# Four small transfers at the head of a matmul with batch norm: 256 words of w, or 64 of w and 64 of x

## The chip, the cores and the metric

The kernel runs on one core of one Trainium2 chip. The metric is the device time of one execution in microseconds, the median of several. The engines are TensorE (PE, its weight loads PEld), VectorE (DVE), ScalarE (ACT), GpSimd (POOL) and SyncE (SP). SyncE, ScalarE and GpSimd can each issue DMA transfers from a queue of their own; sixteen DMA engines carry out what all queues hold.

## The reference

`x` is 16 x 512 x 1024, `weight` (w below) is 1024 x 768, both float32 in HBM; gamma and beta have 768 elements.

```python
y = np.matmul(x, weight)
mean = np.mean(y, axis=(0, 1), keepdims=True)
var = np.var(y, axis=(0, 1), keepdims=True)
y_norm = (y - mean) / np.sqrt(var + eps)
return (gamma * y_norm + beta).astype(np.float32)
```

The statistics go over all 8192 rows, for each of the 768 columns. So no value can be stored before all of its column has been multiplied.

## The kernel before

**Tiling.** The 8192 rows of x are 16 chunks of 512 rows; the 768 columns are six tiles of 128. The contraction of 1024 is cut into four quarters of 256. Quarter `i` of w lies on partitions `32*i` to `32*i+31`, as bfloat16; each partition holds `JW` = 4 groups (`jw`) of two neighbouring rows of w. x is loaded the same way: `load_x` (L395) sends one transfer for each quarter of the contraction, to the 32 partitions of that quarter, and VectorE turns the data with STREAM_TRANSPOSE (L428, L435) so that TensorE can contract over the partitions. Both kinds of load convert float32 to bfloat16 on the way and go through GpSimd's queue.

**Order.** Most work is emitted as tasks with a due time; `arrange` (L122) puts them into one order for each engine with estimated durations, and `seq` (L293) pins that order. The loads come in a list written by hand (L440): `("x", 0), ("w", 0, 2), ("x", 1), ("w", 2, 4)`, the next two pieces of 256 rows of x, then whole chunks of 512 rows. `BETWEEN = {0: [0, 1]}` moves the first two quarters of the first w piece ahead of the x quarters of the first piece. So GpSimd issues: quarters 0 and 1 of w (`jw` 0 and 1, that is the first 128 rows of each 256), four quarters of x rows 0 to 255, quarters 2 and 3 of w, four quarters of x rows 256 to 511, four quarters of w (`jw` 2 and 3), and so on. The first eight are issued at once; each later one waits for the landing of an earlier transfer. A w transfer is 64 packets and an x transfer of 256 rows is 256, over the sixteen DMA engines.

**The first products.** TensorE begins with idle matmuls (L591, L594) that fill its time. The first product (L510, columns 0 to 255, x as the stationary operand) needs the first piece of x, turned, and all four quarters of the first w piece. Then L575 multiplies with w stationary. The next products need x rows 256 to 511, and after them the second w piece.

**The lines of the change.** Ahead of all tasks the kernel fills a few constants with VectorE, lets ScalarE compute one square root (L346, which loads ScalarE's function table), and issues four small transfers from SyncE (L347 to L350) into the tile `touched`, which nothing reads:

```python
seq(nc.scalar.activation(warm, eps_sb, AF.Sqrt))
touched = singles.tile([P, 2, TOUCH], f32)
first_rows = weight.rearrange("(i jw c e) n -> i c jw (e n)", i=4, jw=JW, e=2)
for i in range(4):
    seq(nc.sync.dma_start(touched[32 * i:32 * i + 32, 0:2], first_rows[i, :, 0:2, 0:TOUCH]))
```

Each of the four reads 64 single words of one quarter of w: word 0 of every second row of that quarter's first 128 rows. These are the rows that the first w piece begins its descriptors with. `load_quarter` (L386) issues the transfers of w proper, with the same arrangement.

Of the kernel before, what the change touches and what calls it, by code (L numbers as in the profile page):

```python
# [227 lines left out]
def kernel(  # L228
# [9 lines left out]
    nc = tc.nc  # L238
    f32 = mybir.dt.float32
# [8 lines left out]
    P = 128  # L248
# [7 lines left out]
    JW = KQ // 64  # L256
# [4 lines left out]
    TOUCH = 1  # L261
# [20 lines left out]
    x_flat = x.flatten_outer_dims()  # L282
    out_flat = out.flatten_outer_dims()

    singles = ctx.enter_context(tc.tile_pool(name="singles", bufs=1))
# [7 lines left out]
    def seq(bi):  # L293

        ins = bi.ins
        prev = last.get(ins.engine)
        if prev is not None:
            tc.add_manual_dep(
                ins, prev,
                mybir.DependencyInfo(mybir.DependencyClass.NoSync, mybir.DependencyReason.DATA),  # L300
                reason="order",
            )
        last[ins.engine] = ins.name
        return bi
# [38 lines left out]
    base = singles.tile([P, 2], f32)  # L343
    fss = singles.tile([P, 2], f32)

    seq(nc.scalar.activation(warm, eps_sb, AF.Sqrt))  # L346
    touched = singles.tile([P, 2, TOUCH], f32)  # L347
    first_rows = weight.rearrange("(i jw c e) n -> i c jw (e n)", i=4, jw=JW, e=2)
    for i in range(4):
        seq(nc.sync.dma_start(touched[32 * i:32 * i + 32, 0:2], first_rows[i, :, 0:2, 0:TOUCH]))  # L350


    tasks, turns = [], {}
# [88 lines left out]
    at = M - CH  # L442
# [5 lines left out]
    for kind, n, *n1 in order:  # L448
# [24 lines left out]
        for i in range(rows // QR):  # L473
            c, q = divmod(m0 // QR + i, QPC)
# [9 lines left out]
        if rows % QR:  # L484
            t0 = rows // QR * QR // 32
            m1 = m0 + 32 * t0
            c, q = divmod(m1 // QR, QPC)
# [851 lines left out]
    for c, r0, rows in ends:  # L1339
        due = E + 2.0 + 0.6 * c  # L1340
        n = max(rows // CH, 1)
# [70 lines left out]
```

## Time and profile before

| what | value |
|---|---|
| median of 3 runs (lowest to highest) | 205.74 us (205.7 to 206.15) |
| span of the profiled execution | 204.1 us |
| its own end-to-end time | not given; the median is 1.64 us above the span |
| PE busy, share of the span | 189.3 us, 93% |
| DVE, ACT, POOL busy | 159.3, 146.2, 124.1 us |
| granted TensorE clock, mean | 0.979 |
| queue q0 (GpSimd's loads): packets, MB | 34624, 18.36 |
| queue q1 (SyncE's transfers): packets, MB | 63920, 30.16 |
| the four small transfers, issue to landing | 1.6 to 4.1 us, median 2.6 |

Times are from one profiled execution. Bytes are counted as they are written, so a load that converts to bfloat16 counts half of what it reads. A chain of waits follows the end of the kernel back, at each step to what released the waiting work. In the timeline a row has its start, its length, the engine, the line, the operation and how many of them it merges; in brackets stands the idle time before it and what ended it.

### The profile page before, as it was taken

The numbers are of one execution on the slowest core, as the hardware profiler recorded it, in microseconds if no ns is written. First come the engines' busy times: TensorE is split into PE (matmuls) and PEld (weight loads), VectorE is DVE, ScalarE is ACT, GpSimd is POOL, SyncE is SP. The second block draws the span as 40 slices with busy tenths as digits, with TensorE's granted clock in tenths as the row PEclk, the third lists the DMA queues.
The fourth block names the chain that finished last, engine by engine and source line by source line (L and its number), as shares of the span: only waits on it lengthen the run. The fifth ranks groups of instructions, "written<-read, shape, count | busy, mean of one in ns | idle before, by whom it ended". The sixth has DMA issues, their size and how long they took to land.

```text
span 204.1 us, 3510 instructions
## 1 busy us (share of the span) xinstructions
PE 189.3 (93%) x1210; PEld 114.5 (56%) x1210; DVE 159.3 (78%) x250; ACT 146.2 (72%) x260; POOL 124.1 (61%) x150
## 2 busy tenths in 40 slices
PE   7969999999999999999999999999999999997900
PEld 3457554657488888777865444444444445544600
DVE  4031879999999999969989998987999878657900
ACT  2001461368989999899978766999998959956950
POOL 7776954877499989997403999389613312940000
PEclk9999999999999999999999999999999999999965
DMA  4999999999999999999686899899999999999998
GB/s 71 172 199 196 176 196 196 196 197 197 190 193 197 197 196 196 196 197 195 103 181 200 297 339 336 248 301 328 295 322 227 336 303 274 347 343 310 310 347 253
DMA packets 98562, 48.74 MB, mean 239 GB/s; under 512 B 24304, under 2 KB 98032, under 8 KB 98544
## 3 DMA queue, kind: packets, MB, share of 16 engines
q0 software_dynamic: 34624, 18.36, 65.5%
q1 hardware_dynamic: 63920, 30.16, 52.6%
q8 instruction: 9, 0.15, 0.3%
q14 instruction: 9, 0.07, 0.1%
HBM read 36.71 MB, written 25.17 MB: 303 GB/s over the span
## 4 chain that ended last, share of the span: by engine, by line
PE 86%; ACT 3%; DMA 3%; POOL 2%; issue 1%; ACTq 0%; DVE 0%; POOLq 0%
PE y_ps L575 54%; PE y_ps L510 24%; PE y_ps L814 4%; ACT o_sb L1361 3%; DMA ring<-in_x_dram 3%; PE o_ps L1044 1%; POOL ring L403 1%; POOL w_sb L387 1%; PE y_ps L753 1%; PE a_ps L903 1%; PE o_ps L1074 0%; ACTq L1407 0%; PE idle_ps L591 0%; PE tot_ps L871 0%; ACT ring L1252 0%
## 5 line engine op out<-in xcount | busy, mean ns | idle before, releaser
L575 PEld LDWEIGHTS <-w_sb 128*128 128x128 bf16 x520 | 50.3, 97 | 57.6
L575 PE MATMUL y_ps<-xT_sb,w_sb 128*128 128x512 bf16 (+1 forms) x272 | 59.3, 371 | 0.0
L575 PE MATMUL y_ps<-x_pl,w_sb 128*128 128x512 bf16 x248 | 57.4, 379 | 0.0
L403 POOL DMA_DIRECT2D ring<-in_x_dram x76 | 47.2, 626 | 14.4 <-DMA ring<-in_x_dram 5.5
L510 PE MATMUL y_ps<-w_sb,xT_sb 128*128 128x256 bf16 x448 | 50.6, 273 | 1.7 <-DMA ring<-in_x_dram 1.6
L510 PEld LDWEIGHTS <-xT_sb 128*128 128x128 bf16 x448 | 43.5, 98 | 9.4 <-DVE xT_sb L435 2.9
L435 DVE STREAM_TRANSPOSE xT_sb<-ring 128x1024 f32<-128x1024 f32 (+1 forms) x29 | 31.2, 1111 | 14.1 <-DMA ring<-in_x_dram 13.9
L711 DVE BATCH_NORM_STATS2 stats<-y_ps 128x6 f32<-128x512 f32 x46 | 30.9, 687 | 7.7 <-PE y_ps L575 7.2
L715 ACT CAST y_sb<-y_ps 128x512 bf16<-128x512 f32 x51 | 29.0, 593 | 10.4 <-DVE stats L711 6.3
L547 ACT COPY x_pl<-xT_sb 128x1024 bf16<-128x1024 bf16 x32 | 32.8, 1063 | 1.7 <-DVE xT_sb L435 1.7
L942 POOL TENSOR_TENSOR ring<-ring,sum 128x1024 f32<-128x1024 f32 (+1 forms) x11 | 23.8, 2188 | 14.9 <-ACT y_ps L724 10.9
L659 ACT ACTIVATE sq_sb<-y_ps 128x512 f32<-128x512 f32 x28 | 16.3, 610 | 16.2 <-PE y_ps L510 15.9
L666 POOL TENSOR_TENSOR sum<-sum,sq_sb 128x512 f32<-128x512 f32 x20 | 25.6, 1278 | 3.0 <-ACT sq_sb L659 1.7
L662 DVE TENSOR_TENSOR sum<-y_ps,sum 128x512 f32<-128x512 f32 x28 | 18.9, 675 | 6.3 <-ACT sq_sb L659 5.3
L672 ACT CAST y_sb<-y_ps 128x512 bf16<-128x512 f32 x28 | 16.3, 594 | 8.2 <-DVE sum L662 8.0
L1178 POOL TENSOR_TENSOR ring<-ring,sum 128x1024 f32<-128x1024 f32 x6 | 14.8, 2477 | 9.8 <-issue 8.5
L937 DVE TENSOR_TENSOR ring<-y_sb,a_ps 128x1024 f32<-128x1024 bf16 (+1 forms) x16 | 16.7, 1079 | 0.1
L1044 PE MATMUL o_ps<-ident,y_sb 128*128 128x128 bf16 x104 | 13.1, 221 | 1.6 <-DVE y_sb L1348 1.5
L1232 ACT CAST ring<-ring 128x1024 f32<-128x1024 bf16 x13 | 13.8, 1063 | 0.6 <-DMA ring<-y_sb 0.6
L1145 POOL COPY sum<-sum 32x256 f32<-32x256 f32 (+1 forms) x17 | 5.8, 340 | 13.4 <-DVE sum L1142 6.5
L428 DVE STREAM_TRANSPOSE xT_sb<-ring 128x2048 bf16<-128x2048 bf16 x6 | 13.5, 2290 | 0.1
L591 PE MATMUL idle_ps<-idle_sb 128*128 128x512 f32 x18 | 9.6, 688 | 1.5 <-DVE idle_sb L316 1.5
(104 smaller groups left out, 153.7 us busy)
## 6 DMA issues: line engine op xcount, KB each, us to landing
out_dram<-ring SPq DMA_DIRECT2D x37, 512.0 KB, 3.4
ring<-in_x_dram POOLq DMA_DIRECT2D x52, 256.0 KB, 8.8
out_dram<-o_sb SPq DMA_DIRECT2D x6, 512.0 KB, 4.7
ring<-in_x_dram POOLq DMA_DIRECT2D x16, 128.0 KB, 5.9
w_sb<-in_weight_dram POOLq DMA_DIRECT2D x8, 192.0 KB, 6.2
out_dram<-ring SPq DMA_DIRECT2D x6, 256.0 KB, 3.0
ring<-in_x_dram POOLq DMA_DIRECT2D x4, 192.0 KB, 7.8
out_dram<-o_sb SPq DMA_DIRECT2D x3, 256.0 KB, 2.5
```

The source lines that it names most:

```text
L403: bi = seq(nc.gpsimd.dma_start(x_bf[32 * i:32 * i + 32], src[:, :, KQ * i:KQ * (i + 1)]))
L435: seq(nc.vector.transpose(dst, src[:, :, jw0:jw1]))
L510: seq(nc.tensor.matmul(y_ps[:, s], x_of(c, jw, e, t * P, (t + 1) * P), w_sb[:, jw, e, 0:NA], start=(s == 0 and jw == 0 and e == 0), stop=( ...
L547: seq(nc.scalar.copy(dst, pairs) if eng == "ACT" else ENG[eng].tensor_copy(dst, pairs))
L575: seq(nc.tensor.matmul(y_ps, w_sb[:, jw, e, nt * P:(nt + 1) * P], moving(c, jw, e, q0 * QR, q1 * QR, parted), start=(jw == 0 and e == 0 an ...
L659: seq(nc.scalar.activation(sq_sb[:, 0:n], slot.tile[:, 0:n], AF.Square))
L662: seq(nc.vector.tensor_add(sum1, slot.tile[:, 0:n], sum1))
L666: seq(ENG[eng].tensor_add(acc, acc, state["sq"][:, 0:n]))
L711: seq(nc.vector.bn_stats(dst, slot.tile))
L715: seq(nc.scalar.copy(y(nt, c), slot.tile))
L937: seq(nc.vector.tensor_mul(slot.o, y_row[c].y[:, s0:s1], aff[0][:, None, :].to_broadcast([P, n, NA])))
L942: seq(ENG[eng].tensor_add(slot.o, slot.o, row[:, None, :].to_broadcast([P, n, NA])))
```

## The change

The four small transfers from SyncE go. In their place come two, issued before ScalarE's square root: SyncE reads 64 words of w and ScalarE's own queue 64 words of x, each into one column of the first 64 partitions of `touched`. In both, the words are word 0 of every sixteenth row of rows 0 to 1023: for w that is the whole matrix (48 KB from word to word), for x the first two chunks (64 KB from word to word). The rearrangement sets the sixteen steps within a block of 256 rows (`e`) outermost and the four blocks (`h`) inside. Nothing reads `touched` in either kernel.

```diff
@@ -343,11 +343,11 @@
     base = singles.tile([P, 2], f32)
     fss = singles.tile([P, 2], f32)
 
+    touched = singles.tile([P, 2], f32)
+    for eng, src, at in ((nc.sync, weight, 0), (nc.scalar, x_flat, 1)):
+        words = src[0:1024, 0:1].rearrange("(h e s) n -> e h (s n)", h=4, e=16)
+        seq(eng.dma_start(touched[0:64, at:at + 1], words[:, :, 0:1]))
     seq(nc.scalar.activation(warm, eps_sb, AF.Sqrt))
-    touched = singles.tile([P, 2, TOUCH], f32)
-    first_rows = weight.rearrange("(i jw c e) n -> i c jw (e n)", i=4, jw=JW, e=2)
-    for i in range(4):
-        seq(nc.sync.dma_start(touched[32 * i:32 * i + 32, 0:2], first_rows[i, :, 0:2, 0:TOUCH]))
```

## The prediction

> **What bounds the kernel now.** I read the chain of waits first, because it says which work the end can be followed back to, then the timeline of the head, then the head in windows of 0.5 us, and last the single DMA packets and landings in the trace. The chain, cut to its first 30 us (start, length, what):
>
> ```profile
> 5.98 6.13 DMA ring<-in_x_dram
> 12.11 0.03 issue
> 12.14 1.03 PE y_ps L510 x8
> ...
> 14.99 0.86 PE idle_ps L591 x2
> 15.85 0.87 PE y_ps L510 x8
> 16.72 1.81 PE y_ps L575 x16
> 18.54 0.07 issue
> 18.61 1.91 PE y_ps L510 x16
> ```
>
> From 12.14 us to 184.8 us nearly every later piece of the chain is TensorE work, back to back. Ahead of it stands the wait for the loads. So two clocks rule: until 18.6 us TensorE goes on only as transfers land (at 12.14, 15.68 and 18.61), and from then on as fast as it can multiply. A microsecond won or lost in the landings of the head is a microsecond of the whole kernel, as long as every later landing moves with it. It does: the load queue always has up to eight transfers outstanding, and GpSimd issues each next one about 0.3 us after the oldest has landed (8.38 after 8.09, 9.06 after 8.77, 9.80 after 9.51).
>
> The timeline of the head, with what the change touches (start, length, engine, line):
>
> ```profile
> 0.73 1.28 ACT L346 ACT_TABLE_LOAD   x1 [0.73 <-PEq L1393]
> 0.74 1.81 SPq L350 DMA_DIRECT2D touched<-in_weight_dram  x4
> 1.30 1.21 POOL L387 DMA_DIRECT2D w_sb<-in_weight_dram  x2 [0.85 <-POOLq L1393]
> 2.51 2.29 POOL L403 DMA_DIRECT2D ring<-in_x_dram  x4
> 4.79 1.06 POOL L387 DMA_DIRECT2D w_sb<-in_weight_dram  x2
> 7.00 0.30 ACT L457 CAST ident<-ident 128x128 f32<-128x128 bf16 x1 [4.77 <-POOL ident masks.py:199]
> 10.26 1.30 DVE L435 STREAM_TRANSPOSE xT_sb<-ring 128x512 f32<-128x512 f32 x2 [7.13 <-DMA ring<-in_x_dram]
> ```
>
> No instruction reads `touched`, so the four small transfers can act only through the DMA engines and HBM. The eight large ones behind them are two quarters of w, four of x, two of w. In the trace they land at 4.99, 6.02; 8.09, 8.77, 9.51, 10.14; 11.06, 12.01 us. The transposes begin 0.12 us after the fourth quarter of x, and TensorE 0.13 us after the last quarter of w. Except at the third of them, x quarters follow each other by 0.63 to 0.74 us and w quarters by 0.92 to 1.03. The first quarter of x comes 2.07 us after the w quarter before it, about 1.4 more than its like. The windows show the same hole (the last number is GB/s, the one before it the DMA share):
>
> ```profile
> 5.50:6.00 0.50, 0.50 (x2) 0.19 (x1) 0.00 (x0) 0.00 (x0) 0.50 (x3) 1.00 1.35 167
> 6.00:6.50 0.50, 0.50 (x2) 0.19 (x1) 0.00 (x0) 0.00 (x0) 0.50 (x2) 1.00 0.59 64
> 6.50:7.00 0.50, 0.50 (x3) 0.24 (x2) 0.00 (x0) 0.00 (x1) 0.42 (x3) 1.00 1.04 118
> 7.00:7.50 0.50, 0.50 (x3) 0.26 (x2) 0.00 (x0) 0.30 (x1) 0.48 (x1) 1.00 1.30 169
> 11.00:11.50 0.50, 0.00 (x0) 0.00 (x0) 0.50 (x1) 0.00 (x0) 0.15 (x1) 1.00 1.43 197
> ```
>
> Eleven microseconds in, x streams at 197 GB/s; when x is read for the first time it runs at 64 to 169 for 2 us. This is what a word of x, read ahead, could take away.
>
> **The change, part by part.**
>
> Issue slots. SyncE issues one transfer where it issued four of 0.40 to 0.43 us: 1.2 us less, worth nothing, because its next transfer waits tens of microseconds for DVE (46.2 us in the waits of its queue). ScalarE gets one DMA issue ahead of its table load, about 0.41 us by the four SyncE rows; the table load and the `warm` activation move from 0.73–2.2 to about 1.15–2.65 us. The cover is ScalarE's idle time until 7.00, of which 4.77 us are a wait for `ident`; some 4.3 us of it are left. Without that cover it would cost 0.41. At the end of the kernel one more queue may have to be waited for; a semaphore wait there takes 0.02 to 0.05 us, below what can be seen.
>
> Removed words. Touches three and four are underway during the first two w quarters: 160 of their packets, 8 data words and 2 completions an engine, start after 2.55 us. The sixteen engines finish the two quarters 0.96 us apart with them, and the last two w quarters 0.94 us apart without them. So taking them away is worth 0.00 to 0.04 us; I take 0. What they warm: the old words sit on every second row of the first 128 rows of each w quarter, the new ones on every sixteenth row of all of w. The second halves of the quarters have no touch at all now, and their packets take 247 to 248 ns when first read, as in the steady state. So a sparser cover of w should cost nothing.
>
> The first w packets. Twelve packets that begin between 2.69 and 3.14 us take 460 to 992 ns instead of 247, although words of their rows had been read by 2.54 us. That is some 0.6 us lost, and the w touch does not prevent it. In the changed kernel nothing is queued beside these packets. The price of this part lies between −0.6 (the third touch stood in their way) and +0.6 (more of them, should the thinner cover matter); I take 0, since nothing in the first two touches differs from what stays.
>
> The x words. They leave ScalarE at about 0.74 us. The first SyncE touch had its first packet 1.0 us after its issue and landed at 2.32 us, so the x words are done by about 2.4, before the first w packet at 2.69. If the first read of x is what is dear, it is paid there, where no load is yet moving. What that brings, from three rows. (a) One engine lags: of the sixteen completions of the first x quarter fifteen come by 6.66 and the last at 8.09; this engine stays 0.55 us behind the others up to the landing at 12.01 (the others by 11.45). If only its lag goes, 0.55 us. (b) Mean loss: against 195 GB/s the four windows miss 28 + 131 + 77 + 26 = 262 GB/s over 0.5 us each, 131 KB, which is 0.67 us of streaming. (c) All of the slip goes: the first x quarter then lands with its fifteen early engines, at about 6.7, 1.4 us sooner, and the last w quarter at 10.6; the fillers of TensorE end at 10.56, so all 1.4 would be used. I take (b), 0.67 us: fifteen engines passed the first x quarter without delay and stalled in the second, which reads the same rows, so I doubt that a touch cures the whole.
>
> The sum: 0 for the issue slots, 0 for the w words, 0 for the first w packets, −0.67 for x. The profiled execution spans 204.1 us; its own end-to-end time is not given, and 205.74 − 204.1 = 1.64 us lie around the span, which nothing here touches. The median becomes 205.74 − 0.67 = 205.07, so 205.1 us.
>
> **A rule against it.** In the trace the stall has the size of 0.1 to 0.7 us on single 512-byte packets (371, 738 and 693 ns are the longest, against 60). The Trainium skill, HBM Reference, Latency, knows no dearer first access: 0.2 us on average, 2 us at high load. By that rule there is nothing to warm, the hole is a matter of load, and the sum would be 0 (205.7 us). The recovery to 197 GB/s under the same load speaks against it; the stall on packets of rows already being read speaks for it. I carry its consequence as the first rival.
>
> **The rivals.**
>
> Nothing to warm (0.27). The hole at 6 us is not a first read. For: fifteen engines got through the first x quarter in 0.7 us, and a similar hole stands at 22.5 to 24.5 us, where 39 packets of x are slow, while rows 256 to 1023, first read in between, show none. Against: the first slow packet, at 5.28 us, is one of the first of x, and nothing else in the records starts there (GpSimd's `ident` work begins at 5.84). The result is 205.7, within 0.2% (0.41 us, about what a measurement of this kernel can tell from no change).
>
> The x words block w (0.20, slower). A slow read holds an engine for both queues: between 2.54 and 3.51 us only one packet of the touches moves while the first w packets crawl. If the x words meet what the lagging engine met, 1.4 us, they hold their engines from 1.75 to about 3.2, 0.5 us into the w packets; and if the hole at 6 us stays all the same, the kernel ends 0.5 later, at 206.25. It decides for this when the x words land after 2.7 us and the first x quarter still follows its w quarter by 2 us. Against: the w touches, just as new, took 0.25 us for 80 packets.
>
> The thinner w cover matters (0.08, slower). The third and fourth w quarters, whose words were touched on their own rows, would then begin with packets of 0.8 us: +0.6, 206.3. The untouched half quarters at 247 ns speak against it.
>
> **How the numbers follow.** The forecast, that x is warmed, has 0.45, with its own range 204.3 (c) to 205.2 (a). Faster by over 0.2% means below 205.33: all of this case. Within 0.2% is the first rival, 0.27; slower the other two, 0.28. The range must hold eight in ten: it takes the forecast from (c), 204.3, through the first rival and up to the slow cases at 206.25 and 206.3. What is left out is a gain in both the x hole and the first w packets together (below 204) and a slow case with a dearer stall than any here.
>
> **What would show it.** Right: the x words land by about 2.5 us; the windows between 5.5 and 7.5 us show over 150 GB/s throughout; the first x quarter follows its w quarter by under 1.4 us instead of 2.07; TensorE's first L510 matmul starts near 11.5 instead of 12.14, and the matmuls at 15.68 and 18.61 come as much earlier. Wrong: the hole stays at 64 GB/s near 6 us with the first matmul at 12.1 (nothing to warm); first w packets beginning after 2.7 or a first w landing after 5.0 (blocked); slow packets at the third w quarter (thin cover); or a head that is 0.67 earlier while a later wait, for the x rows that land at 24.3 us, gives it back.

## The result: slower by 0.9 us, and the profile after

The changed kernel takes 206.8 us (median of 17 runs, 206.42 to 208.33) against 206.06 us for the kernel before (17 runs); the ratio is 1.0043, 95% interval 1.0028 to 1.0057, so about 0.9 us (0.6 to 1.2); the two medians alone are 0.74 apart. A later set on one chip gave 207.06 against 205.82, ratio 1.0061 (1.0040 to 1.0082). The forecast was a gain of 0.67 us, to 205.1: wrong in sign. The profiled execution after spans 204.7 us (run of 206.52), that of before 204.1. One execution of an experiment below, the profiled one of the kernel in plain order, took 291.7 us at a granted clock of 0.65 and is left out of the ratio; of its trace only the landings of the head, SyncE's stop and the drain are read.

The chain of waits of the changed kernel, first 30 us (start, length, what):

```profile
5.32 6.85 DMA w_sb<-in_weight_dram
12.17 0.28 issue
12.45 6.18 DMA w_sb<-in_weight_dram
18.64 0.28 issue
18.92 5.87 DMA ring<-in_x_dram
24.80 0.03 issue
...
26.22 1.92 PE y_ps L510 x16
```

In the chain of the kernel before, the same products stand at 25.93:

```profile
25.93 1.92 PE y_ps L510 x16
```

Two things are to be seen. The last w quarter lands at 12.17 instead of 12.01. And the start of TensorE's unbroken work, 25.93 us before, is now 26.22, when a piece of x has landed at 24.80 and has been turned. From there to 184 us the products stay 0.29 or 0.30 us late.

The timeline of the head (start, length, engine, line, operation):

```profile
0.74 0.64 ACTq L349 DMA_DIRECT2D touched<-in_x_dram  x1
0.74 0.69 SPq L349 DMA_DIRECT2D touched<-in_weight_dram  x1
1.41 1.28 ACT L350 ACT_TABLE_LOAD   x1 [1.41 <-PEq L1393]
7.02 0.30 ACT L457 CAST ident<-ident 128x128 f32<-128x128 bf16 x1 [4.11 <-POOL ident masks.py:199]
```

Each of the two new issues takes 0.64 to 0.69 us, not 0.41. The x words land at 2.90 us and the w words at 3.80. The table load moves to 1.41, and the cast that follows stays at 7.02 (7.00 before): ScalarE's slot is hidden. The eight large transfers land at 4.76, 7.00; 8.09, 8.94, 9.62, 10.36; 11.26, 12.17. The windows of the changed kernel (DMA share, then GB/s, at the end):

```profile
5.50:6.00 0.50, 0.50 (x2) 0.19 (x1) 0.00 (x0) 0.00 (x0) 0.50 (x3) 1.00 0.49 46
6.00:6.50 0.50, 0.50 (x2) 0.19 (x1) 0.00 (x0) 0.00 (x0) 0.50 (x2) 1.00 0.58 62
6.50:7.00 0.50, 0.50 (x3) 0.23 (x2) 0.00 (x0) 0.00 (x0) 0.42 (x2) 1.00 0.78 97
7.00:7.50 0.50, 0.50 (x3) 0.26 (x2) 0.00 (x0) 0.30 (x1) 0.22 (x1) 1.00 1.18 151
```

The hole of x is as deep as before, 46 to 151 GB/s against 64 to 169. But 0.29 us of TensorE is not 0.9 us. To see where the rest is, each profiled execution below is cut in three, all against the profiled execution of before: **products** (the end of TensorE's last y_ps product, 186.62 us before), **stores** (the last DMA landing, 203.15 before, less the shift of the products), and **drain** (from the last landing to the end of the span, 0.92 before). For the changed kernel they are +0.29, +0.22 and +0.13.

### The profile page after: what moved, and what is told of

The parts are those of the page before. It is cut to its first block, busy times and chain, and to the rows that moved or that the text cites. A ratio compares the mean times of both kernels' runs of the same rounds, so it can differ in the third digit from the quotient of the medians.

```text
span 204.7 us, 3507 instructions
## 1 busy us (share of the span) xinstructions
PE 189.3 (92%) x1210; PEld 114.5 (56%) x1210; DVE 159.2 (78%) x250; ACT 146.2 (71%) x260; POOL 124.3 (61%) x150
## 4 chain that ended last, share of the span: by engine, by line
PE 79%; DMA 9%; ACT 3%; POOL 2%; DVE 1%; issue 1%; ACTq 0%; DVEq 0%; POOLq 0%
PE y_ps L575 50%; PE y_ps L510 21%; DMA w_sb<-in_weight_dram 6%; PE y_ps L814 4%; ACT o_sb L1361 3%; DMA ring<-in_x_dram 3%; PE o_ps L1044 1%; POOL ring L403 1%; PE y_ps L753 1%; POOL w_sb L387 1%; DVE xT_sb L435 1%; PE a_ps L903 1%; PE o_ps L1074 0%; ACTq L1407 0%; PE tot_ps L871 0%
## 5 line engine op out<-in xcount | busy, mean ns | idle before, releaser
L510 PE MATMUL y_ps<-w_sb,xT_sb 128*128 128x256 bf16 x448 | 50.6, 273 | 2.0 <-DMA ring<-in_x_dram 1.7
L510 PEld LDWEIGHTS <-xT_sb 128*128 128x128 bf16 x448 | 43.4, 98 | 9.8 <-DVE xT_sb L435 3.2
```

Source lines behind the costliest of these rows:

```text
L510: seq(nc.tensor.matmul(y_ps[:, s], x_of(c, jw, e, t * P, (t + 1) * P), w_sb[:, jw, e, 0:NA], start=(s == 0 and jw == 0 and e == 0), stop=( ...
```

## The experiments

Theories at the start: the old words warm the rows they lie on (cover); small transfers help whatever they read (count, or traffic); the word of x does harm or good (x word); and, after the first runs, the place of the tiles in SBUF (placement) and the form of the new transfers (shape).

**None at all**, and the tile gone as well.

```diff
-    touched = singles.tile([P, 2, TOUCH], f32)
-    first_rows = weight.rearrange("(i jw c e) n -> i c jw (e n)", i=4, jw=JW, e=2)
-    for i in range(4):
-        seq(nc.sync.dma_start(touched[32 * i:32 * i + 32, 0:2], first_rows[i, :, 0:2, 0:TOUCH]))
```

> All four small transfers are left out and nothing is put in their place. Cover theory (a word read ahead spares the DMA engine that will load its rows the slow first packets): both the first and the second w quarter begin with packets of 0.4 to 1.2 us instead of 0.25, the second w quarter lands at 7 us or later instead of 6.02, and the kernel is slower than before by at least as much as the changed one, 0.7 us or more. Traffic theory (what helps is that small transfers are in flight between 1.7 and 5.6 us, whatever they read): the same, 0.7 or more. x-word theory (the x word, or the queue it comes from, does the harm): no statement beyond the value of the w words; slower than before by some amount.

**The old four and the word of x.**

```diff
+    touched_x = singles.tile([P, 2], f32)
+    for eng, src, at in ((nc.scalar, x_flat, 1),):
+        words = src[0:1024, 0:1].rearrange("(h e s) n -> e h (s n)", h=4, e=16)
+        seq(eng.dma_start(touched_x[0:64, at:at + 1], words[:, :, 0:1]))
     seq(nc.scalar.activation(warm, eps_sb, AF.Sqrt))
```

> The four w transfers of before stay as they are, and the x word transfer of the changed kernel is added on ScalarE's queue. Cover theory: same as before within 0.3 us, or up to 0.7 faster if the x words spare anything. Traffic theory: same as before within 0.3. x-word theory: slower than before by 0.6 to 0.9 us, as the changed kernel is.

**The new w words without the word of x.**

```diff
-    for eng, src, at in ((nc.sync, weight, 0), (nc.scalar, x_flat, 1)):
+    for eng, src, at in ((nc.sync, weight, 0),):
```

> The changed kernel without its x transfer: one transfer of 64 sparse words of w from SyncE. Cover theory: slow packets of 0.4 to 1.2 us at the second w quarter stay, slower than before by 0.6 to 0.9 us. Traffic theory: the same, 0.6 to 0.9. x-word theory: same as before within 0.3 us, and no slow packets at the second w quarter.

**The old four, reading far words**: x rows 4096 to 5119, which the first 12 us never use.

```diff
-    first_rows = weight.rearrange("(i jw c e) n -> i c jw (e n)", i=4, jw=JW, e=2)
+    far_rows = x_flat[4096:5120].rearrange("(i jw c e) n -> i c jw (e n)", i=4, jw=JW, e=2)
```

> The four small transfers of before, same shape, queue and time, but they read words of x rows 4096 to 5119, which are loaded only some 50 us later, in place of w rows. Cover theory: as without any touch: the second w quarter begins with packets of 0.4 to 1.2 us and the kernel is 0.7 us or more slower than before. Traffic theory: same as before within 0.3 us. x-word theory: same as before within 0.3 us, as no x word comes from ScalarE's queue.

Measured against 205.88: none 208.88, ratio 1.016 (1.0137 to 1.0184); the old four and x 209.06, 1.0149 (1.0130 to 1.0167); new w alone 207.3, 1.0063 (1.0049 to 1.0078); far words 205.85, 0.9997 (0.9985 to 1.0009).

Far words do all that near words do, so it does not matter which rows are read ahead: cover falls. Without the word of x the loss stays, so the x word is not what slows. The first two are spoilt by something else. Both change what the tile takes in SBUF, and the program then places the tiles behind it 32 bytes off a multiple of 512 bytes (in all other kernels here they lie on multiples of 512). The transposing transfers inside SBUF (L1106) suffer. Windows of before, then of the run with none (last number GB/s):

```profile
106.00:106.50 0.50, 0.50 (x4) 0.10 (x1) 0.35 (x3) 0.50 (x3) 0.00 (x0) 1.00 1.19 265
107.00:107.50 0.50, 0.50 (x7) 0.50 (x6) 0.50 (x2) 0.23 (x2) 0.00 (x0) 1.00 1.25 285
```

```profile
106.50:107.00 0.50, 0.50 (x4) 0.17 (x2) 0.40 (x4) 0.50 (x3) 0.00 (x0) 1.00 1.14 209
107.00:107.50 0.50, 0.50 (x6) 0.50 (x7) 0.46 (x3) 0.49 (x2) 0.00 (x0) 1.00 1.10 202
```

Between 106 and 109 us the busiest windows reach 209 GB/s instead of 285 (208 in the run with the old four and x, 270 to 292 in the kernels whose tiles stay in place, the one in plain order aside), and the stores lose 2.6 us in both runs. The Trainium skill (DMA: Bandwidth & Descriptors, How a descriptor splits into AXI transactions) says that the first transaction of a descriptor that does not start on a multiple of 256 bytes starts at the boundary below, and that the bytes before the start are fetched unused. Worked out from this, a 256-byte packet 32 bytes off takes two transactions instead of one. The trace agrees in direction: between 105 and 109 us 17 and 14% of the 256-byte packets took over 25 ns in these two runs, none before and at most 4% in any other of them, though most of them stayed at 18 ns in all.

So the next four keep the tiles in place.

**None, but the tile is still allocated** (the tile's line stays, the loop goes).

> No small transfer at all, but the tile for them is still allocated, so that every later tile of SBUF starts where it starts in the kernel before, at multiples of 512 bytes (without that tile they start 32 bytes lower, as in the first run without transfers). Placement theory (the large losses of the two runs whose tiles moved by 32 bytes come from transposing DMAs that run at some 210 instead of 290 GB/s): transposes at 290 GB/s again, and 0.5 to 1.7 us slower than before instead of 3.0. Theory that the transfers themselves carry the whole 3.0 us: again 2.7 to 3.3 slower. Count theory (each of the four small transfers in flight beside the first loads shortens the slow start): slower than the run with a single transfer, so 1.3 to 1.7.

**The old four and the word of x, its tile 512 bytes long** (`[P, 128]` instead of `[P, 2]`).

> The four w transfers of before and the x transfer from ScalarE's queue, with the x words in a tile of 512 bytes a partition, so that all later tiles stay at multiples of 512. Placement theory: same as before within 0.4 us. x-word theory (a word of x ahead from ScalarE's queue does harm): slower by 0.6 us or more, with 3 us if the whole earlier loss was the x word's. If the x words spare anything, faster by 0.3 to 0.7.

**The first two of the four**, and **the first one of the four** (`range(2)`, `range(1)` instead of `range(4)`).

> Only the first two of the four w transfers of before. Count theory: between before and the run without any, 0.4 to 1.0 us slower, with slow packets (over 0.4 us) at the second w quarter, as no small transfer is in flight after 2.9 us. Shape theory (what the changed kernel lost is that its sparse transfer has its first packet at 2.2 to 2.4 us, not 1.75, just ahead of the loads): same as before within 0.3 us.

> Only the first of the four w transfers of before: as many words and transfers as in the run with the sparse w transfer alone, but in the old shape, with its first packet at 1.75 us. Count theory: 1.0 to 1.6 us slower than before, like that run (1.3 slower). Shape theory: same as before within 0.3 us.

Measured against 205.75: none 207.03, 1.0061 (1.0044 to 1.0079); four and x 206.42, 1.0035 (1.0022 to 1.0049); two 207.46, 1.0080 (1.0066 to 1.0094); one 206.96, 1.0061 (1.0039 to 1.0082).

Placement is confirmed: none with the tile takes 207.03, none without it 208.88, and the old four and x take 206.42 and 209.06. Against the kernel before of its own set, that is 1.7 us in the first pair and 2.5 in the second. The times do not follow the count: two are no better than none or one. The run with two tells where to search. Its products are only 0.04 us late, but its stores 1.42 us and its drain 0.13. A change at 1 us that leaves 180 us of products alone and costs 1.4 us in the stores points to something that is counted.

Two such things are in the traces. The first is the **drain**. Transfers of SyncE and ScalarE take eight completion semaphores (counters that a transfer raises as it lands) in turn, and at the end SyncE waits for the eight in a fixed order; a wait that still follows the one of the last transfer costs about 0.06 us. Before, 88 transfers end on the last semaphore. Over all profiled executions the drain goes by the number of transfers alone: 0.92 or 0.93 us with 88 or 96, 1.04 with 86, 1.10 or 1.11 with 85, 1.17 with 84, 1.35 with 89. That explains most of the 0.67 us of the old four and x, which should have cost under 0.4: 0.43 is its drain, and its products are 0.14 late and its stores not at all. The second is a **hole in SyncE's stream**. In the profiled execution of every kernel here SyncE stands still for 0.44 to 0.47 us (or longer, where its next work is not ready) behind its 79th record, counted from the start of the span (transfers, semaphore waits and drains are records). From here on, "the hole" is this one; that of the x loads is called the hole of x. SyncE's timeline in the kernel before:

```profile
143.07 0.37 SPq L1202 DMA_DIRECT2D out_dram<-ring  x1
143.99 0.37 SPq L1182 DMA_DIRECT2D out_dram<-ring  x1
144.46 1.92 SPq L1220 DMA_TRANSPOSE ring<-y_sb  x1
146.47 0.53 SPq L1202 DMA_DIRECT2D out_dram<-ring  x1
```

and in the changed one:

```profile
143.37 0.37 SPq L1202 DMA_DIRECT2D out_dram<-ring  x1
143.85 0.52 SPq L1182 DMA_DIRECT2D out_dram<-ring  x1
144.47 2.08 SPq L1220 DMA_TRANSPOSE ring<-y_sb  x1
147.10 0.38 SPq L1202 DMA_DIRECT2D out_dram<-ring  x1
```

Before, record 79 is the store at 143.07, and the hole (143.44 to 143.91) stands ahead of the store at L1182. GpSimd finishes that store's data at 143.51, so it leaves some 0.4 us late. Four records fewer, three issues and one semaphore wait, and record 79 is the transpose at 144.47: the hole (146.56 to 147.02) stands ahead of the next store. The L1182 store leaves at once, and the store behind the transpose leaves 0.63 later where the products are 0.29 later. Record 79 is what the next four runs move, with small transfers issued at about 55 us, when SyncE has nothing to do until 100 us.

**The changed kernel and two small transfers late.**

```diff
             seq(nc.sync.dma_start(beta_sb[:, nt:nt + 1], beta[nt * P:(nt + 1) * P, None]))
+        for i in (2, 3):
+            seq(nc.sync.dma_start(touched[32 * i:32 * i + 32].rearrange("p (a n) -> p a n", n=TOUCH), first_rows[i, :, 0:2, 0:TOUCH]))
```

> The changed kernel, and two small transfers (the old third and fourth, 64 words of w each) issued by SyncE at about 55 us, behind the beta loads. Seen in every kernel so far: SyncE stands still for 0.44 to 0.46 us after the 79th instruction that its record shows, whatever that instruction is. Before, this hole falls ahead of the 42nd transfer behind the small ones (L1182, 143.5 to 143.9 us), in the changed kernel behind the 43rd, and 0.2 to 1.4 us are then lost in the stores. Hole theory: the count decides. Two more instructions put the hole back to within one record or two of its old place, four small transfers in all make the last transfer use the last of eight completion semaphores again (drain 0.01 instead of 0.08 us), and what is left is the later head, 0.29 us: 206.0 to 206.2, ratio about 1.0015. Head theory (all that is lost comes out of the head, the store stage only shows it): 206.6 as the changed kernel, ratio 1.004.

**Two at the head, the other two late**; **all four late**; **the kernel before and eight more late** (the same lines with `(2, 3)`, `range(4)` and `(0, 1, 2, 3) * 2`).

> Two of the four old transfers at the head, as in the run with two (207.46, ratio 1.008, its first 144 us only 0.04 later than before); the other two issued by SyncE at about 55 us. Hole theory: SyncE's 79th recorded instruction is the old one again, so the hole is back ahead of L1182 at 143.5 us and the store stage as before: 205.8, ratio 1.000. Head theory (the two transfers are missed at the head): 207.4, ratio 1.008.

> All four old transfers issued by SyncE at about 55 us, none at the head. Hole theory: only what the head loses without any small transfer is left, 0.78 us at TensorE: 206.5, ratio 1.004, and the drain at the end 0.01 us instead of 0.19. Head theory: as without any, 207.0, ratio 1.006. If these small transfers do nothing at the head at all: 205.75.

> The kernel before, and eight more small transfers issued by SyncE at about 55 us (the old four, twice). The head is unchanged. Hole theory: the hole moves eight or more records forward, to between 131 and 137 us, where SyncE waits 0.6 to 1.5 us for its work anyway; the transfer at 143.99 us (L1182) then leaves 0.4 us earlier; twelve small transfers use the same last semaphore as four. 205.4 to 205.75, ratio 0.998 to 1.000. Head theory: no change, 205.75. If eight more transfers cost something by themselves: over 205.75.

Measured against 205.91: changed and two late 207.77, 1.0088 (1.0066 to 1.0110), a miss of 1.6 us; two and two 206.61, 1.0036 (1.0021 to 1.0051), between the two theories; four late 206.38, 1.0031 (1.0013 to 1.0050), close to the 206.5 of the hole theory; before and eight late 205.9, 0.9995 (0.9978 to 1.0011), no change.

The miss belongs to the theory's "within one record or two". Its record 79 is the L1182 store itself, the hole stands ahead of the transpose, and its stores lose 1.55 us: the same place as in the run with two (1.42), and the dearest found. One record decides. Eight late send the hole to 135 us, and nothing is won: ahead of the L1182 store it had cost nothing that shows. In the other two the hole is back ahead of the L1182 transfer, and their stores lose 0.01 and 0.19, their drain 0.01 and 0.00. What remains of their medians, 0.3 to 0.7 us, is put down to the head by elimination. Their traces do not settle it: the products are 0.97 us late with two and two, but 0.06 early with four late.

The next four put the hole against the head.

**The changed kernel and ten late** (`(2, 3, 0, 1) * 2 + (2, 3)`).

> The changed kernel, and ten small transfers issued by SyncE at about 55 us (the old four, two and a half times): twelve small ones in all, so the last transfer uses the last of the eight completion semaphores, and SyncE's hole after its 79th recorded instruction falls ten or more records earlier, before 140 us, where SyncE waits anyway (in the run of before with eight late ones that cost nothing: 205.9 against 205.91). Hole theory: only the changed head is left, 0.3 to 0.5 us: 206.2 to 206.4, ratio 1.0015 to 1.0025, and the last landing no more than 0.2 us later than TensorE's shift. Head theory: as the changed kernel, 206.7 to 206.8, ratio 1.004. If the changed head costs nothing: 205.9.

**The kernel before, its head untouched, with two loads of beta fewer.**

```diff
-        for nt in range(NT):
-            seq(nc.sync.dma_start(beta_sb[:, nt:nt + 1], beta[nt * P:(nt + 1) * P, None]))
+        for nt, n in ((0, 2), (2, 2), (4, 1), (5, 1)):
+            seq(nc.sync.dma_start(beta_sb[:, nt:nt + n], beta[nt * P:(nt + n) * P].rearrange("(t p) -> p t", p=P)))
```

> The kernel before with its four small transfers, but beta loaded at about 51 us by four transfers instead of six (two pairs). The head is untouched. Hole theory: SyncE's 79th recorded instruction is two records later in the program, ahead of the 43rd transfer behind the small ones (L1220), where the hole cost 1.4 to 1.5 us in the run with two at the head and in the changed kernel with two late ones; the drain costs 0.12 us more. 207.2 to 207.5, ratio 1.007 to 1.008. Head theory: the head is that of before, so 205.9, ratio 1.000 (1.0005 with the drain).

**Twelve at the head.**

```diff
+    for at, rows, jw in ((0, x_rows, 0), (2, first_rows, 2)):
+        for i in range(4):
+            seq(nc.sync.dma_start(more[32 * i:32 * i + 32, at:at + 2].rearrange("p (a n) -> p a n", n=1), rows[i, :, jw:jw + 2, 0:1]))
```

> The kernel before, with eight more small transfers from SyncE right behind the four at the head: 256 words of x rows 0 to 255 of each block of 256 (as the old four do in w), and 256 words of the second half of each w quarter. They are issued until about 6.2 us. The last completion semaphore is that of before, the hole falls as early as in the run of before with eight late ones, which cost nothing. If the head wants small transfers whatever they read (count theory: none cost 0.5 to 1.3 us, four far ones did as well as four near ones): 205.4 to 205.9. If x must be read ahead to be fast (x-word theory): first x quarter at 6.7 instead of 8.09, 205.2. If small transfers between the loads hold these up: above 206.3.

**The changed kernel, its words in plain order.**

```diff
-        words = src[0:1024, 0:1].rearrange("(h e s) n -> e h (s n)", h=4, e=16)
-        seq(eng.dma_start(touched[0:64, at:at + 1], words[:, :, 0:1]))
+        words = src[0:1024, 0:1].rearrange("(r s) n -> r (s n)", s=16)
+        seq(eng.dma_start(touched[0:64, at:at + 1], words[:, 0:1]))
```

> The changed kernel with the same 128 words in plain order (partition p takes word 0 of row 16 p) instead of steps outermost and blocks inside. Shape theory: the issue takes 0.4 us instead of 0.64 and 0.69, the words land by about 2.4 instead of 2.90 and 3.80 us, the first w packets are no longer held up, and 0.2 to 0.5 us of the head come back: 206.3 to 206.6, ratio 1.002 to 1.0035. Otherwise as the changed kernel: 206.7 to 206.8, ratio 1.004.

Measured against 205.91: ten late 206.58, 1.0019 (1.0000 to 1.0037); two loads of beta fewer 207.3, 1.0059 (1.0042 to 1.0077); twelve at the head 205.97, 0.9997 (0.9980 to 1.0014); plain order 207.04, 1.0046 (1.0024 to 1.0069).

The second shows that a loss of this size needs no change at the head. Nothing ahead of 48 us is changed, and the kernel is 1.4 us slower by the medians (1.2 by the ratio), as the hole theory had forecast. SyncE's timeline there has its gap between the L1182 store and the transpose, 144.34 to 144.80:

```profile
143.35 0.37 SPq L1202 DMA_DIRECT2D out_dram<-ring  x1
143.82 0.52 SPq L1182 DMA_DIRECT2D out_dram<-ring  x1
144.87 1.73 SPq L1220 DMA_TRANSPOSE ring<-y_sb  x1
```

Its profiled execution was one of its fastest (206.62; products +0.28, stores +0.34, drain +0.13), so the loss in the stores was 0.3 to 1.5 us in the three profiled executions with the hole at this place. How 0.45 us becomes 1.5 was not followed through the stores. Ten late leave the stores at 0.02 and the drain at 0.01: the changed head alone is worth about 0.4 (0.0 to 0.8); its 206.58 lies between the 206.4 and 206.7 that the two theories had forecast. Twelve at the head are the kernel before: the head does not want more. They do not test x read ahead, because the first of their x words land at 6.73 us, beside the first x quarter (the x quarters land at 7.72, 9.16, 9.84, 10.51). In plain order the words land earlier, at 2.68 and 3.00 us, for nothing: the form is no cause.

The last two, on one chip, divide the loss: **the kernel before with four loads fewer** (beta in three pairs, one more pair of gamma), its hole where the changed kernel has it, and **the changed kernel again**.

> The kernel before with its four small transfers at the head, but gamma and beta loaded at about 50 us by seven transfers instead of eleven. SyncE's 79th recorded instruction is four records later in the program, as in the changed kernel: the hole falls behind the 43rd transfer behind the small ones (L1220), ahead of the 44th (L1202). The last transfer uses the completion semaphore of the run with none (drain 0.25 us later than before, the changed kernel's 0.12). Hole theory, from the stores of the runs with this place of the hole (0.1 to 0.6 lost): 206.2 to 206.7, ratio 1.002 to 1.004. Head theory: 205.9 to 206.1, ratio 1.000 to 1.001 (the drain).

> The changed kernel as it is, once more, beside the run with four loads less. If hole and drain are all that the change costs: within 0.2 us of that run. If the head has its part: 0.3 to 0.7 us above it. By its own earlier times 206.8, ratio 1.004.

Measured against 205.82: four loads fewer 206.54, 1.0026 (1.0012 to 1.0039); the changed kernel 207.06, 1.0061. Both parts exist: by the ratio, hole and drain cost 0.54 us here (0.25 to 0.8; 0.13 of it because its drain is longer than the changed kernel's, 1.17 against 1.04), so about 0.4 of the changed kernel's loss is theirs. The rest, 0.85 of 1.26 in this set and 0.5 of 0.9 in the first, is then the head's; by the medians the changed kernel lies 0.52 above the run with four loads fewer, within the 0.3 to 0.7 expected for a part of the head. This is a subtraction: it takes the hole to cost the same in both kernels, which is not shown, and the intervals leave the rest anywhere between about 0.2 and 1.5. The profiled execution with four loads fewer also shows what a faster head is worth. Its chain:

```profile
5.33 6.23 DMA w_sb<-in_weight_dram
11.55 0.28 issue
...
18.54 6.25 DMA ring<-in_x_dram
24.80 0.03 issue
...
26.22 1.92 PE y_ps L510 x16
```

Here the first x quarter landed at 6.38 us, 1.7 us earlier than before, the last w quarter at 11.55, and TensorE's first L510 product began at 11.69, 0.45 earlier. Yet the piece of x that starts the unbroken work landed at 24.80, as in the changed kernel, and TensorE was 0.29 late from 26.22 on. The gain was gone by the second hole of x, between 22.5 and 24.5 us. (Another 0.27 us went at 105 to 110 us, where its chain runs through VectorE, so its products end 0.57 late; its stores are 0.10 and its drain 0.25 late. Why the chain went there was not followed.)

No kernel was faster than the one before; far words, eight late and twelve at the head equal it.

## Why the prediction was wrong, step by step

Forecast and result lie about 1.5 us apart, a gain of 0.67 against a loss of 0.9. Three parts make this up: the x words brought none of their 0.67; the issue slots with the end of the kernel, put at nothing, cost about 0.4; the removed words, put at nothing, cost what is left, about 0.5, by subtraction.

**Issue slots: a term put at nothing for the wrong reason.** The prediction gave SyncE's missing issues "worth nothing", with the wait of 46 us as cover. As time they are covered. But the stream also lost four records, and a fixed stop of 0.45 us after 79 records moved from ahead of a store, where it cost nothing, to behind a transpose. Stores and drain together cost about 0.4 us (0.54 less 0.13, from the run with four loads fewer), 0.35 in the profiled execution of after and 1.08 in that of the second set. The trace of before had the gap (143.44 to 143.91); nothing in it told that it is bound to a count.

**The end of the kernel: mis-sized.** "0.02 to 0.05 us" for one more queue was 0.13, and not for the queue: the last of 86 transfers lies two semaphores earlier in the turn than the last of 88.

**The x words: the largest term, and it fell.** The term of −0.67 needed the hole at 6 us to be a first read that a word of x could pay. The words landed at 2.90 instead of 2.4, still ahead of the first x packets, and the windows stayed at 46 to 151 GB/s. In plain order they landed at 2.68 us, and the first x quarter came at 8.02. What makes the hole of x stays open. And the working assumed that a landing won in the head is won for the whole kernel; the chain of the run with four loads fewer shows 0.45 us won at 11.7 and lost by 24.8. The prediction named that last danger among its signs and gave it no chance.

**Removed words, thinner cover, first w packets: right on the addresses, wrong on the sum.** Far words cost nothing, so rows do not matter. Yet with hole and drain out of the way, heads with fewer than the four transfers lost 0.7 us (two at the head, 1.0036), 0.6 (none, 1.0031) and 0.4 (the changed one, 1.0019, whose interval reaches down to no loss), where heads with four or twelve lost nothing (0.9997, 0.9995, 0.9997). So the step that gave the removed words 0.00 to 0.04 us failed. Where in the head this arises, and by what mechanism, stays open. TensorE's first product begins at 11.69 to 12.59 us in eight executions with the four or more, mean 12.31, and at 12.05 to 12.89 in eleven without, mean 12.44. The products end on average 0.30 us late in the eight and 0.46 in the eleven. One execution of each cannot show a difference of 0.5.

**The ScalarE issue: mechanism right, size off.** 0.64 us instead of 0.41, hidden as forecast (7.02 against 7.00).

**The rivals.** "Nothing to warm" was right about x and wrong about the time. "The x words block w" decides at an x landing after 2.7 us with the first x quarter still 2 us behind its w quarter; the landing came at 2.90, but the first w quarter landed at 4.76, earlier than before, the x quarter came 1.09 us behind its w quarter, and leaving the x word out did not help. By those 1.09 us a sign of being right was met, but for another reason: the w quarter was late (7.00 instead of 6.02), and the x quarter came at 8.09 as before. "Thinner cover" falls with the far words. None of the four cases held the stores, so the range ended 0.5 us too low.

## What to carry to other kernels

Adding or taking away an instruction early in a queue shifts everything on that queue that goes by count: in this kernel a 0.45 us stop after a fixed number of records and the turn of eight completion semaphores. Before believing that an edit at the head helps or harms, compare the shift of the products at the end with the shift of the last landing; if they differ, search late. And repeat an edit with dummies that restore the count, and with the tiles kept at their addresses, before its effect is put down to what it does.

## What was not expected of the hardware

- SyncE's stop: 0.44 to 0.47 us behind the 79th record in the profiled execution of each of these kernels, followed 1.3 to 3.0 us later by one 8192-byte packet of the instruction queue q14 (at 145.70 us before, 148.23 after). With eight and ten late this packet moves forward with the stop, to 137.75 and 139.77, while the other eight packets of q14 stay within 1.3 us of their places. That it is the crossing from one block of instructions to the next is inferred from the fixed count and this packet, not shown. The Trainium skill (Runtime: NRT & Kernel Launch, Instruction fetch mechanics) says of such a crossing that its cost is "one DMA tail-bump, mostly hidden". If this is one, the trace disagrees: SyncE stands for 0.45 us, and the place of the stop was worth from nothing to 1.5 us in the stores.
- The drain in steps of about 0.06 us by the number of transfers modulo eight, 0.92 to 1.35 us.
- Tiles 32 bytes off: 209 instead of 285 GB/s in the busiest windows of the transposing transfers; 2.6 us in the stores of both profiled executions, 1.7 and 2.5 us by the medians.
- The same head lands its first x quarter at 6.38, 7.99, 8.02 or 8.09 us (four loads fewer, two of beta fewer, eight late, before), and a piece of x behind the second hole, at 22.5 to 24.5 us, lands at 24.3 before and between 23.1 and 25.1 in the other kernels. One profiled execution can't carry a claim of half a microsecond on this head.
